# A hybrid mixer trunk on one core: the first norm's weights spread by TensorE, four weight tiles, convolutions that read a copy

## The chip, the core and the metric

The kernel runs on one core of a Trainium2 chip. Its engines each work through their own list of instructions in order: PE (TensorE: matmuls and transposes), DVE (VectorE), ACT (ScalarE), POOL (GpSimd), and SP (SyncE), which here only issues transfers (DMA). An instruction waits at the head of its engine's list until what it needs is there, and what stands behind it waits too. Matmuls write PSUM, which has eight banks of 128x512 f32; everything else lives in SBUF. The metric is the device time of one execution in microseconds (us), less is better.

## The reference

One layer on 512 tokens of width 1024, in f32:

```
u = rms_norm(x, mix_norm_g)
fa, fb, fc, fd, fg = split(u @ w_in)            # w_in: 1024 x 10528
rwkv7_mix(fa)   gla_mix(fb)   mlstm_mix(fc)     # fc: conv of 4 taps on q, k, then silu
ssd_mix(fd)                                     # z, xbc, dt; xbc: conv of 4 taps, then silu
merged = sum_i sigmoid(fg_i) * (branch_i @ branch_proj_i)
h = x + merged @ w_out
u = rms_norm(h, ffn_norm_g)
gate, val = split(conv3(u @ ffn_up))
out = rms_norm(h + (silu(gate) * val) @ ffn_down, final_norm_g)
```

`rms_norm(x, g)` is `x * rsqrt(mean(x*x) + eps) * g` over the 1024 columns; `g` is one row, the same for all tokens. A convolution of four taps is `y[t] = b + w3 x[t] + w2 x[t-1] + w1 x[t-2] + w0 x[t-3]` for each channel, and silu of it follows.

## The kernel before, in words

Tokens stand in four blocks of 128. The head (lines 287 to 298) loads `x` by block (`xt`), the norm's weights spread over 128 partitions (`g1`, a transfer of 512 KB, line 292), and then, for each block, squares on ACT (line 262), the inverse root on DVE and POOL (lines 247, 248), the product `un` on DVE (line 265), eight transposes on PE (line 269) and the split of the result in two parts, `uh` (a cast on ACT, line 251) and `ul` (the rest, a subtraction on DVE, line 252).

Each dense product with weights is a **split product**: a part of the weights, 128x512, arrives as `raw` (line 222, three buffers, issued by SP), ACT casts it to `hi` (line 225), DVE, or POOL for some, subtracts to `lo` (line 226), and PE does three matmuls for each chunk of 128 rows: lines 235 to 237 (128x512) for outputs that have channels on the partitions, lines 330 to 332 (128x256) for outputs that have tokens there. `hi` and `lo` have three buffers each (line 218). A part lives until its last matmul; then its pair is free for the part three later. Sums of dense products stand in the pool `psd` of three PSUM banks; `psr` (three) and `psm` (two) serve the rest, and `pm()` hands out `psm` or, in some stretches, by a running count, `psr`.

The stages, in the order of the profile: head; first half of rwkv, whose triangular solve is a chain of 62 DVE rows (lines 600, 602) that ends in a transfer to DRAM and back (`mnd`, `MN`) before PE's line 629; gla; the eight convolutions of ssd (`ssd_x`, which calls `conv4`, lines 902 to 912), two or three of them inside the first solve; ssd with its branch and the projection `z` (lines 1084, 1085, which read `psd` and so free its banks); the second half of rwkv with the second solve and the four convolutions of mlstm; mlstm; the output product; the FFN.

`conv4` reads the product's bank: ACT makes the fourth tap with the bias (line 904), three DVE instructions add the other taps (line 907), each with the bank as one input, ACT takes tanh (line 909), DVE finishes silu (line 910). In ssd, for each of four blocks `b`, a transfer spreads a row of cumulated decays over 128 partitions (`sab`, line 1019, 512 KB, two buffers), lines 1022 to 1043 make the decay factors on DVE, ACT and POOL, line 1052 multiplies by the scores, and PE multiplies by the inputs (line 1056).

The order of every engine's list is made by a scheduler that simulates the kernel with its own costs and takes, of the instructions that are ready, the one of highest priority; priorities stand in the table `Q` (lines `P_*`, and `split=800` for the casts and subtractions of weights). So a buffer more, or an instruction more, moves rows far from the edit.

Of the kernel before, what the change touches and what calls it, by code (L numbers as in the profile page):

```python
# [9 lines left out]
F32 = mybir.dt.float32  # L10
F32R = mybir.dt.float32r
AF = mybir.ActivationFunctionType
ALU = mybir.AluOpType
# [3 lines left out]
P = 128  # L17
T = 512
D = 1024
# [141 lines left out]
def kernel(ctx: ExitStack, tc: tile.TileContext, A, out):  # L161
    nc = tc.nc
    V, S, G, PE = nc.vector, nc.scalar, nc.gpsimd, nc.tensor
# [23 lines left out]
    wp = ctx.enter_context(tc.tile_pool(name="wp", bufs=1))  # L187
# [26 lines left out]
    def col(name, i=0, lo=0, hi=P):  # L214
        return pf[lo:hi, PF_AT[name] + i:PF_AT[name] + i + 1]

    def w_tiles():
        return (wp.tile([P, 512], F32R, tag="hi", name="hi", bufs=3), wp.tile([P, 512], F32R, tag="lo", name="lo", bufs=3))

    def split_h(src, h, tiles=None, eng=V):  # L220
        raw = wp.tile([P, 512], F32, tag="raw", name="raw", bufs=NRAW)
# [66 lines left out]
    xt = np_.tile([P, NB, D], F32, name="xt")  # L288
    g1 = np_.tile([P, D], F32, name="g1")
    nc.sync.dma_start(xt[:, 0], x_v[:, 0])  # L290
    nc.sync.dma_start(ident, A["cst"][:, 0:P])
    nc.sync.dma_start(g1, A["gvec"][0:D].partition_broadcast(P))
    for b in range(1, NB):
        nc.sync.dma_start(xt[:, b], x_v[:, b])
    for b in range(NB):
# [42 lines left out]
    def t2(pool=None):  # L338
        pl, n = pool or wpool
        return pl.tile([P, T], F32, tag="w", name="w", bufs=n)  # L340
# [559 lines left out]
        return res  # L900

    def conv4(ps, w, b, n, i, pool=None):
        y = t2(pool)
        S.activation(y, ps, AF.Identity, scale=col(w, 3 * n + i), bias=col(b, i))
        for k in range(3):
            d = 3 - k
            V.scalar_tensor_tensor(y[:, d:T], ps[:, 0:T - d], col(w, k * n + i), y[:, d:T], op0=ALU.mult, op1=ALU.add)  # L907
        th = t2(pool)
        S.activation(th, y, AF.Tanh, scale=0.5)
        V.scalar_tensor_tensor(y, th, 1.0, y, op0=ALU.add, op1=ALU.mult)  # L910
        return y
# [297 lines left out]
    nc.sync.dma_start(gb2, A["gvec"][D:2 * D].partition_broadcast(P))  # L1209
    gb3 = hp.tile([P, D], F32, name="gb3")  # L1210
    nc.sync.dma_start(gb3, A["gvec"][2 * D:3 * D].partition_broadcast(P))
    hw_ctx = ExitStack()
    hw = hw_ctx.enter_context(tc.tile_pool(name="hw", bufs=1, side="right", reuse_waits="tile"))
    wx = [hw.tile([P, 512], F32R, name=n) for n in ("wxh", "wxl")]
    hx = ExitStack()
    np_ = hx.enter_context(tc.tile_pool(name="nq", bufs=1, side="right", reuse_waits="tile"))

# [5 lines left out]
    for b in range(NB):  # L1223
# [3 lines left out]
        for n in range(2):  # L1227
            ps = pd()
            for k in range(KD):
                w = n * 8 + k  # L1230
# [5 lines left out]
        norm_T(h2[:, b], gb2, b, np_, uh, ul, 1, [pr_, pm])  # L1236
    tap("h2", h2)
    hx.close()
    first = fm_halves([(A["up"][0], (None, None)), (A["up"][1], (None, (wx[0], wx[1])))])
    hw_ctx.close()  # L1240
    wo_ctx.close()
    mo_ctx.close()
    ps_ctx.close()
# [91 lines left out]
```

## Time and profile before

| | |
|---|---|
| median of 3 runs | 1195.45 us (1193.54 to 1199.78) |
| profiled execution | 1195.54 us, its span 1193.7 us |
| busy, share of the span | PE 96%, DVE 55%, ACT 37%, POOL 28% |
| mean granted clock of PE | 0.984 of full |
| chain that ended last | PE 74%, DVE 11%, DMA 7%, issue 4%, ACT 2% |
| costliest rows | DVE line 226, 229.0 us; ACT line 225, 199.6 us; PE lines 235 to 237, 1073.7 us |

The profiled execution is 1.8 us longer than its span (start and end around it). A busy PE counts from a matmul's start to its modelled end, and neighbours overlap, so what PE loses is read from the bracket at the end of a row of the timeline: the idle time before that instruction, and what ended it. The clock column gives the share of full clock that was granted in a stretch.

### The profile page before, as it was taken

Reading aid. Unit: us, or ns where it says so; the run is one execution under the profiler, and the core shown is the slowest. Engines: PE = TensorE matmul, PEld = TensorE weight load, DVE = VectorE, ACT = ScalarE, POOL = GpSimd, SP = SyncE. Lnnn points to the kernel's source line nnn. Section 1 sums busy time; section 2 is a strip of 40 time slices with the busy share of each in tenths; the row PEclk is TensorE's granted clock in tenths of the full one; section 3 lists DMA queues with packets and bytes.
Section 4 is the critical chain, followed back from the end, with each engine's and each line's share of the span. In section 5 each row is a group of like instructions: output and inputs, shape, how many; then the busy total and the mean of one; then the engine's idle time right before and its main releaser. Section 6 shows DMA issues by size and latency. Waiting matters only on the chain.

```text
span 1193.7 us, 17895 instructions
## 1 busy us (share of the span) xinstructions
PE 1143.7 (96%) x6881; PEld 928.9 (78%) x6881; DVE 651.6 (55%) x1090; ACT 444.4 (37%) x820; POOL 331.4 (28%) x287
## 2 busy tenths in 40 slices
PE   5999989999999999989999999999999999999997
PEld 4887868777788767778777777778788888888886
DVE  5258796453576365793235653554665666652323
ACT  4355234332333432232124343432444444442323
POOL 3104012230285543331114543620212222220100
PEclk9999989999998999999999999999999999999999
DMA  5222322322341322332224523561232223222322
GB/s 198 65 98 64 88 61 70 103 78 79 105 98 53 98 80 67 93 83 91 68 84 150 160 88 115 184 201 38 89 101 96 96 96 99 97 97 97 97 97 107
DMA packets 79886, 117.30 MB, mean 98 GB/s; under 512 B 22660, under 2 KB 27172, under 8 KB 79800
## 3 DMA queue, kind: packets, MB, share of 16 engines
q1 hardware_dynamic: 79224, 115.11, 30.6%
q8 instruction: 54, 0.88, 0.3%
q10 hardware_dynamic: 576, 1.05, 0.2%
q14 instruction: 32, 0.26, 0.1%
HBM read 107.93 MB, written 8.19 MB: 97 GB/s over the span
## 4 chain that ended last, share of the span: by engine, by line
PE 74%; DVE 11%; DMA 7%; issue 4%; ACT 2%; POOL 1%; SPq 1%; POOLq 0%; DVEq 0%; ACTq 0%
PE psd L235 17%; PE psd L236 16%; PE psd L237 16%; PE psd L1282 3%; PE psd L1283 3%; PE psd L1284 3%; DVE Mi L602 2%; DVE Mt L600 2%; DMA sab<-ad 2%; DVE lo L226 1%; PE psr L676 1%; PE psd L331 1%; PE psd L330 1%; DMA raw<-in_wo_dram 1%; PE psd L332 1%
## 5 line engine op out<-in xcount | busy, mean ns | idle before, releaser
L226 DVE TENSOR_TENSOR lo<-raw,hi 128x512 fp32r<-128x512 f32 x280 | 229.0, 819 | 312.0 <-ACT hi L225 300.6
L225 ACT CAST hi<-raw 128x512 fp32r<-128x512 f32 x322 | 199.6, 620 | 485.7 <-PE psd L236 300.9
L235 PE MATMUL psd<-uh,hi 128*128 128x512 f32 (+1 forms) x912 | 359.9, 395 | 11.5 <-DVE w L907 4.8
L237 PE MATMUL psd<-uh,lo 128*128 128x512 f32 (+1 forms) x912 | 357.6, 393 | 4.5 <-DVE lo L226 4.1
L236 PE MATMUL psd<-ul,hi 128*128 128x512 f32 (+1 forms) x912 | 356.2, 391 | 0.2 <-DVE ul L252 0.2
L235 PEld LDWEIGHTS psd<-uh,hi 128*128 128x128 f32 x912 | 172.2, 189 | 53.0 <-ACT hi L225 6.2
L237 PEld LDWEIGHTS psd<-uh,lo 128*128 128x128 f32 x912 | 172.2, 189 | 44.8 <-DVE lo L226 5.6
L236 PEld LDWEIGHTS psd<-ul,hi 128*128 128x128 f32 x912 | 172.3, 189 | 36.8 <-issue 2.6
L226 POOL TENSOR_TENSOR lo<-raw,hi 128x512 fp32r<-128x512 f32 x42 | 56.9, 1356 | 194.2 <-ACT hi L225 157.5
L1271 POOL TENSOR_TENSOR y<-y 128x512 f32<-128x512 f32 x22 | 28.3, 1288 | 174.0 <-DVE y L1265 160.1
L1265 DVE SCALAR_TENSOR_TENSOR y<-psd,pf,y 128x510 f32<-128x510 f32 x88 | 65.9, 750 | 2.7
L1284 PE MATMUL psd<-hi,al 128*128 128x512 f32 x164 | 63.8, 389 | 0.0
L1283 PE MATMUL psd<-lo,ah 128*128 128x512 f32 x164 | 63.8, 389 | 0.0
L331 PE MATMUL psd<-lo,uh 128*128 128x256 f32 x192 | 57.1, 298 | 1.0 <-DVE lo L226 1.0
L1282 PE MATMUL psd<-hi,ah 128*128 128x512 f32 x164 | 57.3, 389 | 0.0
L332 PE MATMUL psd<-hi,ul 128*128 128x256 f32 x192 | 56.3, 294 | 0.0
L330 PE MATMUL psd<-hi,uh 128*128 128x256 f32 x192 | 55.8, 292 | 0.0
L331 PEld LDWEIGHTS psd<-lo,uh 128*128 128x128 f32 x192 | 37.8, 197 | 5.2 <-issue 3.3
L332 PEld LDWEIGHTS psd<-hi,ul 128*128 128x128 f32 x192 | 37.9, 197 | 1.3 <-issue 1.0
L330 PEld LDWEIGHTS psd<-hi,uh 128*128 128x128 f32 x192 | 37.7, 197 | 1.6 <-issue 1.2
L1284 PEld LDWEIGHTS psd<-hi,al 128*128 128x128 f32 x164 | 30.8, 188 | 6.5
L1282 PEld LDWEIGHTS psd<-hi,ah 128*128 128x128 f32 x164 | 30.8, 188 | 6.4
(418 smaller groups left out, 1696.5 us busy)
## 6 DMA issues: line engine op xcount, KB each, us to landing
raw<-in_wfm_dram SPq DMA_DIRECT2D x140, 256.0 KB, 2.6
raw<-in_up_dram SPq DMA_DIRECT2D x88, 256.0 KB, 2.5
raw<-in_dn_dram SPq DMA_DIRECT2D x44, 256.0 KB, 2.5
raw<-in_bp_dram SPq DMA_DIRECT2D x32, 256.0 KB, 2.7
raw<-in_wtm_dram SPq DMA_DIRECT2D x24, 256.0 KB, 2.6
raw<-in_wo_dram SPq DMA_DIRECT2D x16, 256.0 KB, 3.0
gd<-th SPq DMA_DIRECT2D x15, 256.0 KB, 2.1
th<-gd SPq DMA_DIRECT2D x15, 256.0 KB, 2.9
```

What stands on the lines that cost most here:

```text
L225: S.copy(hi, raw)
L226: eng.tensor_tensor(lo, raw, hi.bitcast(F32), op=ALU.subtract)
L235: PE.matmul(ps, lh, rh, start=first, stop=False)
L236: PE.matmul(ps, lh, rl, start=False, stop=False)
L237: PE.matmul(ps, ll, rh, start=False, stop=last)
L330: PE.matmul(o, uh[:, k, bs], hi[:, cs], start=first, stop=False)
L331: PE.matmul(o, uh[:, k, bs], lo[:, cs], start=False, stop=False)
L332: PE.matmul(o, ul[:, k, bs], hi[:, cs], start=False, stop=last)
L1265: V.scalar_tensor_tensor(y[:, d:T], ps[:, 0:T - d], col("fcw", k * 44 + n), y[:, d:T], op0=ALU.mult, op1=ALU.add)
L1282: PE.matmul(ps, ah[:, k, bs], hi, start=(k == 0), stop=False)
L1283: PE.matmul(ps, ah[:, k, bs], lo, start=False, stop=False)
L1284: PE.matmul(ps, al[:, k, bs], hi, start=False, stop=(k == NF - 1))
```

## The change

Three edits.

1. The row of the norm's weights comes as one row (`grow`, 4 KB) in place of the spread copy of 512 KB. A row of ones times it, two f32 products on PE, spreads it in two PSUM banks (one of `psd`, one of `psm`), and DVE copies both into `g1`.
2. `hi` and `lo` have four buffers each. The extra pair `wx` that held one part of the FFN's first product is gone; that part takes its tiles from the four.
3. `conv4` copies the bank to SBUF on ACT first (into `th`, the tile that takes the tanh later), and the four taps read the copy. ACT has one more instruction of 128x512 for each of the twelve convolutions; the bank is free after that copy.

```diff
--- before.py
+++ after.py
@@ -215,7 +215,7 @@
         return pf[lo:hi, PF_AT[name] + i:PF_AT[name] + i + 1]
 
     def w_tiles():
-        return (wp.tile([P, 512], F32R, tag="hi", name="hi", bufs=3), wp.tile([P, 512], F32R, tag="lo", name="lo", bufs=3))
+        return (wp.tile([P, 512], F32R, tag="hi", name="hi", bufs=4), wp.tile([P, 512], F32R, tag="lo", name="lo", bufs=4))
 
     def split_h(src, h, tiles=None, eng=V):
         raw = wp.tile([P, 512], F32, tag="raw", name="raw", bufs=NRAW)
@@ -288,8 +288,15 @@
     xt = np_.tile([P, NB, D], F32, name="xt")
     g1 = np_.tile([P, D], F32, name="g1")
     nc.sync.dma_start(xt[:, 0], x_v[:, 0])
+    grow = np_.tile([1, D], F32, name="grow")
+    nc.sync.dma_start(grow, A["gvec"][0:D].partition_broadcast(1))
     nc.sync.dma_start(ident, A["cst"][:, 0:P])
-    nc.sync.dma_start(g1, A["gvec"][0:D].partition_broadcast(P))
+    ones = np_.tile([1, P], F32, name="ones")
+    V.memset(ones, 1.0)
+    for n, bank in enumerate((pd, pm)):
+        ps = bank()
+        PE.matmul(ps, ones, grow[:, n * 512:(n + 1) * 512], start=True, stop=True)
+        V.tensor_copy(g1[:, n * 512:(n + 1) * 512], ps)
     for b in range(1, NB):
         nc.sync.dma_start(xt[:, b], x_v[:, b])
     for b in range(NB):
@@ -900,12 +907,12 @@
         return res
 
     def conv4(ps, w, b, n, i, pool=None):
-        y = t2(pool)
-        S.activation(y, ps, AF.Identity, scale=col(w, 3 * n + i), bias=col(b, i))
+        y, th = t2(pool), t2(pool)
+        S.copy(th, ps)
+        S.activation(y, th, AF.Identity, scale=col(w, 3 * n + i), bias=col(b, i))
         for k in range(3):
             d = 3 - k
-            V.scalar_tensor_tensor(y[:, d:T], ps[:, 0:T - d], col(w, k * n + i), y[:, d:T], op0=ALU.mult, op1=ALU.add)
-        th = t2(pool)
+            V.scalar_tensor_tensor(y[:, d:T], th[:, 0:T - d], col(w, k * n + i), y[:, d:T], op0=ALU.mult, op1=ALU.add)
         S.activation(th, y, AF.Tanh, scale=0.5)
         V.scalar_tensor_tensor(y, th, 1.0, y, op0=ALU.add, op1=ALU.mult)
         return y
@@ -1209,9 +1216,6 @@
     nc.sync.dma_start(gb2, A["gvec"][D:2 * D].partition_broadcast(P))
     gb3 = hp.tile([P, D], F32, name="gb3")
     nc.sync.dma_start(gb3, A["gvec"][2 * D:3 * D].partition_broadcast(P))
-    hw_ctx = ExitStack()
-    hw = hw_ctx.enter_context(tc.tile_pool(name="hw", bufs=1, side="right", reuse_waits="tile"))
-    wx = [hw.tile([P, 512], F32R, name=n) for n in ("wxh", "wxl")]
     hx = ExitStack()
     np_ = hx.enter_context(tc.tile_pool(name="nq", bufs=1, side="right", reuse_waits="tile"))
 
@@ -1236,8 +1240,7 @@
         norm_T(h2[:, b], gb2, b, np_, uh, ul, 1, [pr_, pm])
     tap("h2", h2)
     hx.close()
-    first = fm_halves([(A["up"][0], (None, None)), (A["up"][1], (None, (wx[0], wx[1])))])
-    hw_ctx.close()
+    first = fm_halves([(A["up"][0], (None, None)), (A["up"][1], (None, None))])
     wo_ctx.close()
     mo_ctx.close()
     ps_ctx.close()
```

Below, rows of the engines' lists. Line numbers of after are 7 higher from the head's loop on, names carry other numbers.

The head on DVE (`un` is the normed block, `ul` its low part; `omu` to `dskip` are small constants for later, made from the transfers `pf` and `dskip`). Before:

```order
L265 SCALAR_TENSOR_TENSOR un_144<-xt_89,ss_140,g1_90 128x1024
L265 SCALAR_TENSOR_TENSOR un_165<-xt_89,ss_161,g1_90 128x1024
L252 TENSOR_TENSOR ul_85<-psr_125,uh_84 128x4x128
L354 TENSOR_SCALAR omu_313<-pf_77 128x14
L356 TENSOR_SCALAR hwa_315<-pf_77 128x8
L358 TENSOR_SCALAR oka_317<-pf_77 128x4
L360 TENSOR_SCALAR hng_319<-pf_77 128x1
L361 TENSOR_SCALAR hng_319<-pf_77 128x4
L438 COPY rkb_336<-pf_77 128x256
L351 TENSOR_SCALAR dskip_310<-dskip_310 128x8
```

After:

```order
L265 SCALAR_TENSOR_TENSOR un_111<-xt_89,ss_107,g1_90 128x1024
L265 SCALAR_TENSOR_TENSOR un_132<-xt_89,ss_128,g1_90 128x1024
L247 TENSOR_SCALAR ss_149<-ss_149 128x1
L361 TENSOR_SCALAR omu_322<-pf_77 128x14
L363 TENSOR_SCALAR hwa_324<-pf_77 128x8
L365 TENSOR_SCALAR oka_326<-pf_77 128x4
L367 TENSOR_SCALAR hng_328<-pf_77 128x1
L368 TENSOR_SCALAR hng_328<-pf_77 128x4
L445 COPY rkb_345<-pf_77 128x256
L358 TENSOR_SCALAR dskip_319<-dskip_319 128x8
L265 SCALAR_TENSOR_TENSOR un_153<-xt_89,ss_149,g1_90 128x1024
```

The two copies into `g1` stand ahead of these rows, and the seven rows from `omu` to `dskip`, which stood behind the fourth `un`, now stand ahead of the third.

The middle of ssd on SP (`ad` is the row of decays in DRAM, `sab` its spread copy, the four in order of the blocks; `in_wtm` are the weights of `z`, `in_wfm` those of the next stage). Before:

```order
L1019 DMA sab_2738<-ad_2725 128x8x128
L1019 DMA sab_2795<-ad_2725 128x8x128
L222 DMA raw_3464<-in_wtm_dram 128x512
L222 DMA raw_3470<-in_wtm_dram 128x512
L222 DMA raw_3524<-in_wtm_dram 128x512
L222 DMA raw_3530<-in_wtm_dram 128x512
L222 DMA raw_3594<-in_wtm_dram 128x512
L1019 DMA sab_2858<-ad_2725 128x8x128
L222 DMA raw_3600<-in_wtm_dram 128x512
L222 DMA raw_3654<-in_wtm_dram 128x512
L222 DMA raw_3660<-in_wtm_dram 128x512
L1019 DMA sab_2921<-ad_2725 128x8x128
```

After:

```order
L222 DMA raw_3677<-in_wtm_dram 128x512
L1013 DMA ad_2742<-w_2738 8x512
L1026 DMA sab_2755<-ad_2742 128x8x128
L1026 DMA sab_2812<-ad_2742 128x8x128
L222 DMA raw_3793<-in_wfm_dram 128x512
L222 DMA raw_3799<-in_wfm_dram 128x512
L222 DMA raw_3833<-in_wfm_dram 128x512
L1026 DMA sab_2875<-ad_2742 128x8x128
L1026 DMA sab_2938<-ad_2742 128x8x128
```

The weights of `z` used to be issued between the four `sab`; now all of them stand ahead of `ad`, and the third and fourth `sab` are neighbours.

The same place on DVE (`sf_2923` before and `sf_2940` after are the factors of the fourth block; lines 1085 and 1092 read a bank of `psd` for `z`). Before:

```order
L1050 COPY sbt_2891<-psm_2890 128x256
L1052 SCALAR_TENSOR_TENSOR sab_2858<-psr_2889,sab_2858 128x512 x2
L226 TENSOR_TENSOR lo_3603<-raw_3600,hi_3602 128x512
L1063 TENSOR_TENSOR w_2875<-psr_2910,sf_2860 128x512
L1074 TENSOR_TENSOR w_2918<-w_2918,psr_2915 128x512
L1033 COPY w_2936<-psr_2931 128x512
L1058 TENSOR_TENSOR w_2873<-w_2873,psm_2899 128x512
L1038 TENSOR_TENSOR w_2938<-w_2936,sf_2923 128x512
L1085 SCALAR_TENSOR_TENSOR w_3458<-w_3458,psd_3462 128x256
```

After:

```order
L1031 TENSOR_SCALAR sf_2940<-sf_2940 128x8
L1032 TENSOR_TENSOR sf_2940<-sab_2938,stk_2753 128x8
L1040 COPY w_2953<-psm_2948 128x512
L1048 TENSOR_SCALAR sab_2938<-sab_2938,stk_2753 128x128
L1045 TENSOR_TENSOR w_2955<-w_2953,sf_2940 128x512
L1034 SCALAR_TENSOR_TENSOR sf_2940<-sf_2940,stk_2753 128x8
L1048 TENSOR_SCALAR sab_2938<-sab_2938,stk_2753 128x128 x3
L1092 SCALAR_TENSOR_TENSOR w_3475<-w_3475,psd_3479 128x256
L1092 SCALAR_TENSOR_TENSOR w_3475<-w_3475,psd_3609 128x256
L1102 TENSOR_TENSOR w_2770<-w_2770,w_3475 128x512
L1092 SCALAR_TENSOR_TENSOR w_3476<-w_3476,psd_3479 128x256
L1092 SCALAR_TENSOR_TENSOR w_3477<-w_3477,psd_3480 128x256
```

The first reader of a `z` bank stood behind the third block's line 1052; now it stands right behind the fourth block's factors, and the third block's line 1059 (1052 before) comes behind all of them.

The same place on PE, behind the second block's products with `sab` (line 1056 before, 1063 after). Before:

```order
L1031 MATMUL psr_2868<-cst_76,w_2301 128x128
L1048 MATMUL psr_2889<-w_2436,w_2346 128x128
L1048 MATMUL psr_2889<-w_2481,w_2391 128x128
L331 MATMUL psd_3462<-lo_3527,uh_84 128x256
L332 MATMUL psd_3462<-hi_3526,ul_85 128x256
L330 MATMUL psd_3462<-hi_3526,uh_84 128x256
L331 MATMUL psd_3462<-lo_3527,uh_84 128x256
L332 MATMUL psd_3462<-hi_3526,ul_85 128x256
L330 MATMUL psd_3462<-hi_3526,uh_84 128x256
L331 MATMUL psd_3462<-lo_3527,uh_84 128x256
```

After:

```order
L1063 MATMUL psm_2853<-w_2829,sab_2812 128x64 x4
L1056 MATMUL psm_2907<-cst_76,w_2359 128x128
L1056 MATMUL psm_2907<-cst_76,w_2405 128x128
L1038 MATMUL psm_2948<-cst_76,w_2175 128x128
L1038 MATMUL psm_2948<-cst_76,w_2221 128x128
L1038 MATMUL psm_2948<-cst_76,w_2267 128x128
L1038 MATMUL psm_2948<-cst_76,w_2313 128x128
L1055 MATMUL psm_2969<-w_2451,w_2359 128x128
L1055 MATMUL psm_2969<-w_2497,w_2405 128x128
L337 MATMUL psd_3610<-hi_3613,uh_84 128x256
```

Before, split products of `z` (`psd_3462`) fill the place between the blocks; now only small products do, and the next split product opens a bank of its own, `psd_3610`, after `psd_3479`, `psd_3480` and `psd_3609`, so it needs one of these three freed.

## Rows read from the trace of the kernel before

**Rows 1.** The page, part 2: PE and its clock in 40 slices.

```profile
PE   5999989999999999989999999999999999999997
...
PEclk9999989999998999999999999999999999999999
```

**Rows 2.** Busy time by stretch; columns in the first line.

```profile
core 0: us, PE busy (x) PEld busy (x) DVE busy (x) ACT busy (x) POOL busy (x), PEclk, DMA share, GB/s
...
150.00:165.00 15.00, 10.16 (x128) 7.76 (x127) 14.76 (x30) 5.07 (x9) 3.87 (x3) 0.77 0.15 54
...
300.00:330.00 30.00, 28.67 (x148) 22.12 (x147) 18.03 (x37) 10.34 (x23) 10.28 (x9) 1.00 0.31 98
...
330.00:375.00 45.00, 41.76 (x281) 38.95 (x279) 31.48 (x59) 12.15 (x24) 35.06 (x29) 0.92 0.30 76
...
510.00:525.00 15.00, 12.54 (x48) 9.91 (x47) 14.35 (x27) 3.66 (x6) 6.41 (x5) 0.89 0.25 88
```

**Rows 3.** Waits: who waited for whom, us in total, times, longest.

```profile
ACT hi L225 <- PE psd L236: 300.9, 174, 6.2
```

**Rows 4.** Head, 0 to 25 us: start, duration, instruction, idle before it.

```profile
1.64 0.42 SPq L292 DMA_DIRECT2D g<-in_gvec_dram  x1
...
8.89 1.29 DVE L265 SCALAR_TENSOR_TENSOR un<-xt,ss,g 128x1024 f32<-128x1024 f32 x1 [3.27 <-DMA g<-in_gvec_dram]
...
19.41 0.64 DVE L354 TENSOR_SCALAR omu<-pf 128x14 f32<-128x14 f32 x1
...
23.47 0.15 DVE L351 TENSOR_SCALAR dskip<-dskip 128x8 f32<-128x8 f32 x1
...
10.18 1.06 ACT L262 ACTIVATE sq<-xt 128x1024 f32<-128x1024 f32 x1 [4.76 <-DMA xt<-in_x_dram]
...
24.27 0.39 PE L236 MATMUL psd<-ul,wh 128*128 128x256 f32 x1 [1.29 <-DVE ul L252]
```

**Rows 5.** Line 460: a 128x512 f32 product, as two records; ns min, median, max.

```profile
L460 PE MATMUL psm<-w,cst x8: 592/592/593, 45.7 to 402.9; 128*4 128x512 f32 x8
```

**Rows 6.** PE, matmuls that came late behind a wait for hi or lo.

```profile
94.03 0.39 PE L331 MATMUL psd<-lo,uh 128*128 128x256 f32 x1 [1.02 <-DVE lo L226]
...
328.64 0.50 PE L235 MATMUL psd<-uh,hi 128*128 128x512 f32 x1 [0.76 <-ACT hi L225]
...
441.21 0.54 PE L235 MATMUL psd<-uh,hi 128*128 128x512 f32 x1 [1.77 <-ACT hi L225]
...
502.38 0.50 PE L237 MATMUL psd<-uh,lo 128*128 128x512 f32 x1 [0.88 <-DVE lo L226]
...
516.03 0.50 PE L237 MATMUL psd<-uh,lo 128*128 128x512 f32 x1 [2.46 <-DVE lo L226]
```

**Rows 7.** PE behind the first convolution, and behind the second solve.

```profile
158.72 0.80 PE L235 MATMUL psd<-uh,hi 128*128 128x512 f32 x1 [4.78 <-DVE w L907]
...
533.95 0.22 PE L629 MATMUL psr<-MN,zm 32*32 32x32 f32 x2 [0.62 <-DMA MN<-mnd]
```

**Rows 8.** Lines 907 and 910: duration ns min, median, max, forms.

```profile
L907 DVE SCALAR_TENSOR_TENSOR w<-psd,pf,w x36: 728/748/751, 155.8 to 544.4; 128x509 f32<-128x509 f32 x12, 128x510 f32<-128x510 f32 x12, 128x511 f32<-128x511 f32 x12
...
L910 DVE SCALAR_TENSOR_TENSOR w<-w x12: 657/693/1727, 161.4 to 545.9; 128x512 f32<-128x512 f32 x12
```

**Rows 9.** The solve on DVE, and POOL beside it.

```profile
505.13 0.42 DVE L602 TENSOR_TENSOR Mi<-Mi,Mt 64x256 f32<-64x256 f32 x1
...
507.95 1.40 DVE L600 TENSOR_TENSOR Mt<-Ls,Mi 64x252 f32<-64x252 f32 x1
...
507.60 1.48 POOL L226 TENSOR_TENSOR lo<-raw,hi 128x512 fp32r<-128x512 f32 x1
```

**Rows 10.** SSD: the fourth broadcast of sab, DVE's wait, PE's wait.

```profile
351.45 0.39 SPq L1019 DMA_DIRECT2D sab<-ad  x1
...
357.01 0.99 DVE L1025 TENSOR_TENSOR sf<-sab,stk 128x8 f32<-128x8 f32 x1 [3.34 <-DMA sab<-ad]
...
360.66 1.76 PE L1056 MATMUL psm<-w,sab 128*128 128x64 f32 x7 [3.24 <-DVE sab L1052]
```

## The prediction, made before the run

> **What bounds the kernel now.** I read the page's slices first. PE is at nine tenths nearly everywhere and its clock is full but for single slices [rows 1], so time can be won only where PE idles, in the head, and where a stall is followed by the lower clock level. The stretches come next [rows 2]: from 150 to 165 us PE is busy 10.16 of 15 us at a mean clock of 0.77, from 330 to 375 us 41.76 of 45 at 0.92, from 510 to 525 us 12.54 of 15 at 0.89. The timelines of PE then give the single stalls with what ended them [rows 6, 7, 10]. The waits say what the weights' casts wait for: 300.9 us of ACT's waiting is for a matmul that still reads the pair of three parts before [rows 3]; it is slack of ACT, and costs only where PE then waits for hi or lo. In the last 12 slices PE is at nine tenths or more but for the end [rows 1], with no stall that the change touches, so I give the FFN nothing; that one part takes its tiles from the ring costs nothing either, as the ring is one pair longer.
>
> My sum is made against the profiled execution, 1195.5 us (span 1193.7 and 1.8 around it), which is the median of the runs.
>
> **Edit 1, the head.** It removes a transfer of 512 KB, issued at 1.64 us, whose landing releases the first un at 8.89 us after 3.27 us of waiting by DVE; the second block of x lands at 10.18 us, behind it [rows 4]. It adds a 4 KB transfer, two f32 products (each as two records of 0.59 us, so at most 1.2 us a product [rows 5]) and two copies. A copy of 128x512 from PSUM I take at 0.74 us, from the taps that read PSUM [rows 8]. If the row lands as late as the first un's other input allows (8.89 − 3.27 = 5.6 us is when DVE was idle before), products and copies end at some 7.5 us, and the first un starts 1.4 us earlier; at best the whole 3.27 us is won, and as much again if the blocks of x, which shared the transfer engines with the 512 KB, land earlier too: −4.5. Against it stands the new order on DVE: seven rows from omu to dskip now run ahead of the third un. They took from 19.41 to 23.6 us [rows 4], 4.2 us, and wait for transfers of their own, so the third un loses part of what the first gained. The head's last wait, 1.29 us before 24.27 us, after which PE streams, is for ul, behind the same DVE rows. I take −1.5, with −4.5 and +2 as ends.
>
> **Edit 2, a fourth pair.** Five stalls wait for hi or lo: 1.02 + 0.76 + 1.77 + 0.88 + 2.46 = 6.9 us [rows 6]. A part of weights feeds 12 matmuls, whose records are about 0.5 us long [rows 6] and overlap by some half, so a part lasts about 3 us (an estimate), and the fourth pair lets a cast start that much earlier. Each of the five is shorter than that, so I take all: −7. Where a stall goes, the lower clock behind it may go too: from 510 to 525 us a clock of 0.89 means 15 × 0.11 = 1.7 us of work lost, which makes −8.5 the low end. The other end is 0: two of the five lie inside the second solve, where lo stands in DVE's list among the solve's rows (14.35 of 15 us busy [rows 2]), and a free buffer does not make DVE free.
>
> **Edit 3, the convolutions.** PE waits 4.78 us before 158.72 us because the three taps of the first convolution, behind rows of the solve, still read the bank that the next product needs [rows 7]. ACT's 1.06 us for 128x1024 [rows 4] make some 0.6 us for a copy of half that; with it on ACT, busy 5.07 of 15 us there [rows 2], the bank is free after 0.6 us: 4.8 us gone, and with it the lower clock (15 × 0.23 = 3.45 us of work): −8.2 at most. But PE next needs the solve's result. Before, it waits only 0.62 us for it at 533.95 us [rows 7], so PE and the solve arrive nearly together, and a faster PE waits longer there. By the order DVE runs 104 rows from the solve's first to its last, before 99: three more taps, at 0.75 us each, one more silu row and one more lo, some 3 us more. PE has about 5 us more of dense products ahead of line 629 in the new order, which fills most of that. So of 8.2 us I count −2.5, with −8.2 and +3 as ends. The twelve copies on ACT (7 us in all, ACT 37% busy) are hidden beside PE's products of the next parts; the four of mlstm would cost 4 × 0.6 = 2.4 us where that cover is gone, as PE's line for the scores waits for them.
>
> The taps themselves change one input from PSUM to SBUF. Before, they took 728 to 751 ns, in all 36 cases, while line 910, with two inputs in SBUF, took 657 to 1727 ns [rows 8], and a row of the solve with two SBUF inputs went from 0.42 to 1.40 us while POOL ran beside it [rows 9]. So a tap costs 0.66 us without POOL and up to 1.73 us beside it; POOL is busy 3.87 of 15 us in the first convolutions' stretch [rows 2], so on average it is near 0.9. I keep 0.75 in the sum and give the worse case to a rival. The Trainium skill, SBUF — State Buffer, section "Who interferes with whom", says that a VectorE instruction with two SBUF inputs contends with a GpSimd instruction that reads SBUF, and one with at most one SBUF input doesn't; this trace agrees, by the three rows just named, and by that rule the edit puts 36 instructions under contention that were free of it. Its page VectorE: DVE Perf Modes, section "Rules for kernel authors", says the opposite for a case like this: copy PSUM to SBUF first if many operations follow. No row here has that gain beyond 0.09 us a tap, 3 us of DVE in all.
>
> **What moves: ssd.** This is the largest term, and none of the edits is made there. Before, PE has work of z between the blocks: from 300 to 375 us it idles 1.3 + 3.2 us [rows 2], nearly all of it 3.24 us before 360.66 us, where the third block waits for line 1052, which stands behind a factor of the fourth block, which waits for the fourth sab (issued 351.45, landed 357.01, 5.6 us) [rows 10]. In the new order the weights of z are loaded ahead of the decays, their products are mostly done when the second block's products with sab run, and behind these PE has eight small products and then needs a bank that holds z. Its readers on DVE and ACT stand behind the fourth block's factors, so behind the fourth sab, which can be issued only when the second block's buffer is free. That is a chain: issue and landing 5.6 to 6 us, the factor 0.2 to 1.0 us, the decays and the other rows ahead of the first reader 2 to 3 us, readers of the bank 1 to 2 us: about 10 us in which PE has about 1 us of work. I take 10 us of idle here and 3.5 us before the first block (less of z is left to cover its chain too), 13.5, less the 4.5 of before: +9. The lower clock behind it stands in before as well (45 × 0.08 = 3.6 us of work). Ends: 0 if the order's small products come late enough to be cover themselves, +15 if the first blocks' chains are uncovered too.
>
> **Sum.** −1.5 − 7 − 2.5 + 9 = −2; 1195.5 − 2 = 1193.5 us.
>
> **Rivals.**
> - *The gain stays.* PE reaches ssd later relative to the transfers than I think, and idles there little more than before (+2 in place of +9): −1.5 − 7 − 2.5 + 2 = −9, 1186.5 us. For it: sab's chain begins at the rwkv and gla stage, not at PE, and transfers land in 5.6 us. Against: the z products stand ahead of the blocks by the order, whatever the time.
> - *ssd idles long (the other side).* The fourth sab's wait holds z's banks, and the first blocks' chains are open as well: +15 there, and the weights' stalls inside the second solve stay (−3.5 in place of −7), the convolutions give 0: −1.5 − 3.5 + 15 = +10, 1205.5 us. It decides from some 13 us of added idle between 300 and 375 us. For it: three neighbours on SP and two stages of DVE behind one transfer. Against: before, PE needed only 3.24 us more of that transfer.
> - *Taps beside POOL.* Six taps in the first solve at 1.7 us in place of 0.75 make it 6 us longer, and PE waits for it at line 629: 1193.5 + 6 = 1199.5 us. POOL's share there, a quarter, speaks against all six.
> - *Nothing comes of it*: late weights are DVE's own lateness, the bank's wait turns into the wait for the solve, z finds cover: 1195.5 us.
>
> **How the numbers follow.** Chances: forecast 0.42 (its own range 1187 to 1199), gain stays 0.26 (1179 to 1189), ssd idles long 0.18 (1202 to 1211), taps beside POOL 0.08 (1196 to 1203), nothing 0.06. No measurement of this kernel tells less than 0.5%, 6 us, from no change: faster is below 1189.5, slower above 1201.4. Faster: 0.26 and a fifth of the forecast, 0.35. Slower: 0.18 and a third of the taps, 0.21. The range 1181 to 1206 leaves out the outer third of the second case and of the third.
>
> **What would show it.** Right: first un below 8 us; no wait for hi or lo above 0.5 us before 840 us; no wait of PE for a tap; line 629's first row behind a wait of 2 to 5 us for MN; between 300 and 375 us (about the same work) one idle of PE of 7 to 12 us, ended by a reader of a z bank. Wrong: if that idle is under 4 us the time is below 1189; if it is above 14 us, or the taps' mean is above 1.2 us, it is above 1200.

## The result, and the profile after

The changed kernel takes 1226.86 us (median of 4 runs, 1226.35 to 1229.36) against 1194.49 us before (1192.93 to 1199.78, 4 runs): 2.7% slower, ratio 1.0267 with the 95% interval [1.0232, 1.0303]. The forecast was 1193.5 us in a range of 1181 to 1206, so it was wrong by 33 us; the rival that went the right way, at 1205.5, was 21 us short.

The slices of PE and its clock in the page of after; the twelfth to fifteenth slices (338 to 460 us) stand at 8, 5, 8 and 7, and the clock at 8, 7, 9 and 8. In [rows 1] PE stands at 9 in all four, and the clock too but for an 8 in the thirteenth:

```profile
PE   6998989999985879998999999999999999999997
...
PEclk9998989999987989998999999999999999999999
```

Two groups of dense matmuls (busy, mean ns of one, idle before them and what ended most of it), line 237 before, then lines 235 and 237 from part 5 of the page of after:

```profile
L237 PE MATMUL psd<-uh,lo 128*128 128x512 f32 (+1 forms) x912 | 357.6, 393 | 4.5 <-DVE lo L226 4.1
```

```profile
L235 PE MATMUL psd<-uh,hi 128*128 128x512 f32 (+1 forms) x920 | 362.4, 396 | 15.0 <-DVE w L431 5.8
L237 PE MATMUL psd<-uh,lo 128*128 128x512 f32 (+1 forms) x920 | 359.4, 392 | 1.3 <-DVE lo L226 1.3
```

PE's waits for lo of DVE before line 237 fell to 1.3 us in all (4.1 before), so the fourth pair did what it was to do there. The idle before line 235 has another cause now, line 431, the token shift of rwkv's second half, which reads a bank of dense products.

To see where the time went I took two landmarks that both kernels have: the first half's last chunk of rwkv (line 681 before, 688 after) and the first row of the second half's preparation (line 509, 516). PE's timeline, before and then after:

```profile
302.80 0.40 PE L681 MATMUL psr<-st,kr 64*64 64x64 f32 x8
431.43 1.09 PE L509 MATMUL psr<-wa,wau 64*64 64x512 f32 x8
```

```profile
324.83 0.40 PE L688 MATMUL psr<-st,kr 64*64 64x64 f32 x8
467.39 1.09 PE L516 MATMUL psr<-wa,wau 64*64 64x512 f32 x8
```

The last chunk comes 22.0 us late and the second half 36.0 us late, more than the whole loss; from there on PE wins 2 us back. The split products that PE ran ahead of the second landmark are the same in both (291.9 and 292.1 us of them, by the records of the traces), so these 36 us are lost time and not moved work. The stretch between the landmarks, busy time by engine (columns as in [rows 2]), before and after:

```profile
303.00:431.00 128.00, 123.28 (x685) 104.28 (x680) 73.81 (x134) 47.39 (x98) 69.22 (x56) 0.97 0.31 91
```

```profile
325.00:467.00 142.00, 112.87 (x604) 95.58 (x601) 68.71 (x126) 43.85 (x91) 66.70 (x56) 0.87 0.22 70
```

I price such a stretch as PE's idle time plus its length times what is missing of the clock. Before: 128 − 123.28 = 4.7 and 128 × 0.03 = 3.8, together 8.6 us. After: 142 − 112.87 = 29.1 and 142 × 0.13 = 18.5, together 47.6 us. That is an upper price, as idle time at the lower clock counts in both, but the stretch with these 39 us between them is where the result was made. The single stalls, in PE's timeline of after:

```profile
356.26 0.58 PE L337 MATMUL psd<-hi,uh 128*128 128x256 f32 x1 [5.91 <-DVE mg L418]
...
377.75 0.47 PE L1056 MATMUL psm<-cst,w 128*128 128x128 f32 x1 [3.82 <-DVE w L1065]
...
382.72 0.58 PE L1055 MATMUL psm<-w 128*128 128x128 f32 x1 [2.65 <-DVE w L1040]
...
388.51 0.58 PE L337 MATMUL psd<-hi,uh 128*128 128x256 f32 x1 [4.56 <-DVE w L1092]
...
427.61 0.79 PE L235 MATMUL psd<-uh,hi 128*128 128x512 f32 x1 [3.18 <-DVE w L1092]
...
445.29 0.80 PE L235 MATMUL psd<-uh,hi 128*128 128x512 f32 x1 [5.78 <-DVE w L431]
```

The first four lie ahead of ssd's first block and between its blocks, where before had one stall of 3.24 us [rows 10]. The first, 5.91 us, waits for line 418, which stands in DVE's list behind a wait of 5.01 us for the first `sab`; the fourth is the reader of a `z` bank that the prediction named. The last two lie behind ssd, where the prediction saw nothing. DVE's timeline shows what stood ahead of line 431:

```profile
444.41 0.17 DVE L473 TENSOR_SCALAR nn<-nn 128x16 f32<-128x16 f32 x1 [10.31 <-DMA nn<-nq]
444.49 0.74 DVE L431 SCALAR_TENSOR_TENSOR w<-psd,pf,w 128x511 f32<-128x511 f32 x1
```

Line 431, which frees a bank for the next product, stands in DVE's list behind a row that waits 10.31 us for a transfer to DRAM and back (`nn<-nq`). Before, DVE waited 0.33 us for the same transfer (line 466, at 407.13 us), and PE had no wait above 0.8 us from 361 to 441 us.

The head, on DVE, in order of time, to be set beside [rows 4]:

```profile
6.73 0.69 DVE L299 COPY g<-psd 128x512 f32<-128x512 f32 x1 [1.06 <-PE psd L298]
...
8.39 0.15 DVE L247 TENSOR_SCALAR ss<-ss 128x1 f32<-128x1 f32 x1 [0.96 <-ACT sq L262]
8.46 0.68 DVE L299 COPY g<-psm 128x512 f32<-128x512 f32 x1
9.24 2.48 DVE L265 SCALAR_TENSOR_TENSOR un<-xt,ss,g 128x1024 f32<-128x1024 f32 x2
...
13.43 2.26 DVE L265 SCALAR_TENSOR_TENSOR un<-xt,ss,g 128x1024 f32<-128x1024 f32 x1
```

The first product `un` comes at 9.24 us, not below 8 (8.89 before): the second copy into `g1` stands behind row 247 of the second block, which waits for ACT until 8.39 us. PE was ahead all the same at 40 us: it had done 18.2 us of split products, 16.9 before. Then a new wait of 1.56 us before 59.31 us, for `sg` (line 454), took this back, and by 80 us the head has gained nothing.

### The profile page after: what moved, and what is told of

It reads as the page before. It is cut to its first block, busy times and chain, and to the rows that moved or that the text cites. A ratio compares the mean times of both kernels' runs of the same rounds, so it can differ in the third digit from the quotient of the medians.

```text
span 1227.6 us, 17906 instructions
## 1 busy us (share of the span) xinstructions
PE 1152.6 (94%) x6885; PEld 938.5 (76%) x6885; DVE 658.9 (54%) x1093; ACT 452.4 (37%) x832; POOL 333.5 (27%) x287
## 5 line engine op out<-in xcount | busy, mean ns | idle before, releaser
L235 PEld LDWEIGHTS psd<-uh,hi 128*128 128x128 f32 x920 | 175.2, 191 | 55.5 <-DVE w L431 6.7
L237 PEld LDWEIGHTS psd<-uh,lo 128*128 128x128 f32 x920 | 174.9, 190 | 38.6 <-DVE lo L226 2.2
L236 PEld LDWEIGHTS psd<-ul,hi 128*128 128x128 f32 x920 | 175.3, 190 | 36.7 <-issue 2.1
L337 PE MATMUL psd<-hi,uh 128*128 128x256 f32 x192 | 59.2, 308 | 10.5 <-DVE mg L418 5.9
L1285 PE MATMUL psd<-hi,ah 128*128 128x512 f32 x164 | 63.8, 389 | 0.0
L339 PE MATMUL psd<-hi,ul 128*128 128x256 f32 x192 | 59.4, 310 | 0.0
L337 PEld LDWEIGHTS psd<-hi,uh 128*128 128x128 f32 x192 | 40.3, 210 | 14.3 <-DVE mg L418 6.3
L1286 PEld LDWEIGHTS psd<-lo,ah 128*128 128x128 f32 x164 | 30.8, 188 | 6.4
```

The lines of the kernel that those rows point to most:

```text
L235: PE.matmul(ps, lh, rh, start=first, stop=False)
L236: PE.matmul(ps, lh, rl, start=False, stop=False)
L237: PE.matmul(ps, ll, rh, start=False, stop=last)
L337: PE.matmul(o, uh[:, k, bs], hi[:, cs], start=first, stop=False)
L339: PE.matmul(o, ul[:, k, bs], hi[:, cs], start=False, stop=last)
L1285: PE.matmul(ps, ah[:, k, bs], hi, start=(k == 0), stop=False)
```

## The experiments

Two kinds of numbers recur. The time and its ratio to the kernel before on the same chip (medians of 1195.1 to 1195.9 us there), with the 95% interval in brackets. And the **dense work ahead of the chain**: split products that stand in PE's list ahead of rwkv's last chunk of the first half, counted and priced at the spacing that PE keeps (0.227 us for 128x512, 0.12 us for 128x256). It is 198.9 us before and 217.5 us after; the records of the traces, a few of which are missing, give 198.0 and 216.4.

**Each part alone.** In one line each, from the diff of the change: the head's hunk; the pairs with `wx` gone; `conv4`; the first and the third together.

```diff
+    nc.sync.dma_start(grow, A["gvec"][0:D].partition_broadcast(1))        # head
+        return (wp.tile([P, 512], F32R, tag="hi", name="hi", bufs=4), ...)  # pairs
+        S.copy(th, ps)                                                       # convolutions
```

> Only the head's edit (one row of weights, two products, two copies). Theory A (the fourth pair of weight tiles alone moves the dense products ahead and costs the 32 us): near before, 1190 to 1197 us, and PE starts ssd's last products with sab near 375 us as before. Theory B (the head's additional bank shifts the running count of pm() and so the banks of ssd, which makes the loss): above 1210 us, with the loss between 330 and 450 us.

> Only the four pairs of hi and lo (and no wx). Theory A: the whole loss, 1222 to 1232 us, with some 217 us of dense work in PE's list ahead of the first half of rwkv's last chunk in place of 199, and 20 us or more lost from 330 to 460 us. Theory B (head's banks) or theory C (the convolutions' copy): below 1205 us.

> Only the convolutions' copy. Theory A: near before or a little faster, 1188 to 1197 us: the stall of 4.8 us at the first convolution is gone and the lower clock behind it, part of it comes back at line 629. Theory C (the longer solve and taps beside POOL make the loss): above 1205 us, taps' mean above 1.0 us.

> Head and convolutions, three pairs as before. Theory A: the sum of both alone, 1186 to 1196 us, at least 28 us under the changed kernel. Theories B, C, or that the three edits only lose together: above 1205 us.

Measured: head 1207.82 us (1.0098 [1.0077, 1.0119]), pairs 1229.43 (1.0278 [1.0257, 1.0300]), convolutions 1197.78 (1.0019 [1.0004, 1.0033]), head and convolutions 1202.75 (1.0064 [1.0030, 1.0097]; its runs lie from 1197.06 to 1209.96). The pairs alone make the whole loss. No part wins anything, and they do not add up: +12.5, +34 and +2.5 alone, +32 together. Theory A, that the pairs make the loss, gave the right time for the pairs; its times for the head (to 1197) and for head and convolutions (to 1196) were missed by 11 and 7 us, that for the convolutions by 1. That the head alone costs 12 us is near what B said, and was followed up below.

**What of the pairs costs.** Four pairs, but each part's pair is fixed: every fourth part takes the fourth pair by name (the count starts anew at each stage), where a ring of four gives whichever is free. With head and convolutions, and without:

```diff
+        wn[0] += 1
+        if four[0] and wn[0] % 4 == 0:
+            return (wp.tile([P, 512], F32R, tag="hx", name="hi", bufs=1), ...)
-        return (wp.tile([P, 512], F32R, tag="hi", name="hi", bufs=4), ...)
+        return (wp.tile([P, 512], F32R, tag="hi", name="hi", bufs=3), ...)
```

> All three edits with four pairs, but every fourth part of the weights is given the fourth pair by name, in place of one ring that takes whichever is free. By the order, 201.9 us of dense work then stand ahead of the first half's last chunk of rwkv (198.9 before, 217.5 in the changed kernel). Theory A (the ring of four lets dense products overtake the rwkv chain, and the work is missing later as cover in ssd and behind it): 1198 to 1210 us. Theory D (four pairs cost by themselves, whatever the order: casts and subtractions ahead of the chain on ACT and DVE): 1220 to 1232 us.

> The kernel before with four pairs alone, every fourth part given the fourth pair by name (the head and the convolutions as before). By the order, 201.0 us of dense work stand ahead of the first half's last chunk of rwkv (217.3 with the ring of four, 198.9 before). Theory A (place of the rwkv chain in the dense work): 1194 to 1206 us, at least 23 us under four pairs in one ring (1229.43). Theory D (four pairs cost by themselves): 1220 us or more.

Measured: 1210.15 us (1.0128 [1.0113, 1.0144]) and 1205.15 us (1.0095 [1.0065, 1.0125]): the same number of pairs, 17 and 24 us less than with the ring. Theory D falls for most of the loss, but 10 us stay with the fixed pairs. In the second kernel they are lost by the end of the first solve, not in ssd:

```profile
100.00:120.00 20.00, 17.99 (x83) 12.09 (x84) 10.48 (x18) 7.53 (x12) 3.78 (x5) 0.57 0.10 23
```

The clock is 0.57 there (0.91 before, in the same 20 us). It fell behind a wait of 2.01 us before 102.01 us, and then PE, busy again, ran rwkv's preparation in small products with few dense ones between. This part goes with the fourth pair itself: waits of 1.68 and 2.0 us at 95 to 104 us stand in every kernel whose fourth pair is in use by then, ring or not, and in none with three pairs. Priced as above, from 80 to 130 us these kernels lose 8.0 to 12.9 us, the kernel before 3.5.

Then two kernels that keep the changed kernel's ring of four and all three edits, and change only when some loads of weights may start. In the first the loads of `z` wait for ssd's decays; in the second those of the branch's outputs 4 to 7 and of `z` wait for the rwkv state behind the seventh of eight chunks. Both by a copy of one element into the raw tile ahead of its load:

```diff
         raw = wp.tile([P, 512], F32, tag="raw", name="raw", bufs=NRAW)
+        if gate_:
+            V.tensor_copy(raw[0:1, 0:1], gate_[0])
         nc.sync.dma_start(raw, src[:, 512 * h:512 * h + 512])
```

> The changed kernel, but each load of z's weights waits for the transposed decays of ssd (a copy of one element into the raw tile, from these decays, ahead of each load), so that z's products stand between the blocks of ssd; the rwkv chain's place stays (217.5 us of dense work ahead of it). Theory A: ssd gets cover back and the stalls of 13 us between 366 and 389 us shrink, the wait between the rwkv chain's end and ssd's first block grows: 1212 to 1222 us, 5 to 15 us under the changed kernel. Theory D: no change, 1223 to 1230 us.

> The changed kernel with its ring of four; the loads of weights for the branch's outputs 4 to 7 and for z wait for the rwkv state behind the first half's seventh chunk (a copy of one element of it into the raw tile ahead of each load). By the order 193.7 us of dense work stand ahead of the last chunk, in place of 217.5, and split products of z stand between the blocks of ssd as before. Theory A (the dense work that overtakes the chain is missing as cover in ssd and behind it): 1197 to 1209 us, and from the chain's end to the second half's preparation some 16 to 22 us are lost by PE in place of 47. Theory D (something else that four pairs or the edits bring): 1220 us or more.

Measured: 1225.3 us (1.0265 [1.0226, 1.0304]), no better; and 1208.18 us (1.0119 [1.0085, 1.0153]), 19 us better, in theory A's range. Holding `z` alone leaves the chain where it was in the dense work (217.5 us), and mostly moves the loss: priced as above, 8.7 us more from 330 to 360 us and 11.8 us less from 360 to 390 us. That was a miss of my expectation, and it taught what counts: not which product is kept for ssd, but how much. Holding the branch too brings the chain to 193.7 us of dense work, and it ends at the time of the kernel before (line 691 is 681 there):

```profile
303.57 0.40 PE L691 MATMUL psr<-st,kr 64*64 64x64 f32 x8
```

The same stretch, from the chain's end to the second half's preparation, in this kernel, in the pairs alone, in the fixed pairs alone, and with `z` held:

```profile
304.00:446.00 142.00, 130.81 (x702) 110.73 (x703) 80.30 (x156) 51.19 (x104) 69.86 (x56) 0.95 0.31 94
```

```profile
329.00:469.00 140.00, 114.65 (x616) 97.16 (x614) 66.46 (x126) 44.62 (x91) 68.01 (x56) 0.89 0.25 73
```

```profile
319.00:447.00 128.00, 122.87 (x676) 104.21 (x671) 72.19 (x132) 47.85 (x98) 69.47 (x57) 0.96 0.30 89
```

```profile
325.00:464.00 139.00, 111.08 (x613) 93.50 (x613) 70.68 (x134) 44.40 (x91) 66.88 (x56) 0.90 0.25 76
```

Priced as above: 11.2 + 7.1 = 18.3 us, 25.4 + 15.4 = 40.8, 5.1 + 5.1 = 10.2, 27.9 + 13.9 = 41.8. Set beside the dense work ahead of the chain:

| kernel | dense work ahead | chain ends at | second half at | lost between | time |
|---|---|---|---|---|---|
| before | 198.9 | 303 | 431 | 8.6 | 1195 |
| fixed pairs alone | 201.0 | 319 | 447 | 10.2 | 1205.2 |
| convolutions alone | 198.7 | 312 | 441 | 9.7 | 1197.8 |
| head alone | 198.9 | 309 | 442 | 13.9 | 1207.8 |
| changed, fixed pairs | 201.9 | 313 | 446 | 16.1 | 1210.2 |
| changed, branch and z held | 193.7 | 304 | 446 | 18.3 | 1208.2 |
| pairs in a ring alone | 217.3 | 329 | 469 | 40.8 | 1229.4 |
| changed, z held | 217.5 | 325 | 464 | 41.8 | 1225.3 |
| changed | 217.5 | 325 | 467 | 47.6 | 1226.9 |

The stretches are of one execution, the times are medians; the execution of the changed kernel was its slowest (1229.36), that of `z` held its fastest (1223.3). The three kernels with 217 us lose 41 to 48 us there, all others at most 18. All have run 292 us of dense work by the start of the second half, so what they are late there is lost: 36 us in the changed kernel, 33 and 38 in the other two with 217 us, 10 to 16 in the rest. Behind it some win a part back: from there to the end the table's kernels take 756 to 765 us, the kernel before 762. The kernel with branch and `z` held keeps 12 us of loss although its chain has the least work ahead. They lie in this very stretch: its chain ends 1 us late and its second half starts 15 us late, with 5.2 us of dense work moved into the stretch (198.9 − 193.7) and 9.7 us more lost there (18.3 − 8.6), with waits of 2.65 us for a cast of weights and of 3.59 and 2.84 us in ssd. So the work ahead of the chain separates the two groups and does not order the kernels inside one.

How I read it: a pair that is free lets the scheduler put dense products ahead of chain steps that it takes for not ready. On the chip PE worked through the chain's stretch without idle either way (busy 39.90 of 40 us from 220 to 260 us before, 40.00 after), so the 18.6 us spent there bought nothing, and they are missing where PE waits for transfers: in ssd and behind it.

**The count of banks.** The head draws one more bank from `pm()`, whose running count decides which banks ssd uses. The count alone, in the kernel before; then, with -1 in place of 1, the head without the shift, and head and convolutions without it:

```diff
-    wide, turn = [False], [0]
+    wide, turn = [False], [1]
```

> The kernel before with nothing but the running count of pm() started one higher, as the head's additional bank does; the rest of the work is the same. Theory B in its small form (the count moves the banks of ssd, and this is most of the 12 us that the head's edit alone costs): 1200 to 1207 us, with new stalls between 355 and 370 us. Theory E (the 12 us come from the place of line 629, 116.0 us of dense work ahead of it in place of 111.7): 1193 to 1198 us.

> The head's edit alone with the count of pm() started one lower, so that ssd's banks are handed out as before. Theory E (the head's 12 us come from the place of line 629 and the order behind it, not from banks): 1203 to 1209 us. Theory B: 1194 to 1199 us.

> Head and convolutions, three pairs, and the count of pm() started one lower, so that banks are handed out as before. Dense work ahead of the first half's last chunk is 193.7 us, the least of all orders so far. Theory A: the rwkv chain ends earlier and more cover is left for ssd: 1188 to 1197 us, under head and convolutions with the shifted count (1202.75). Theory E: no better than that, 1199 to 1206 us, as line 629 stands behind 117.6 us of dense work in both.

Measured: 1196.5 us (1.0011 [0.9997, 1.0026]), 1200.18 us (1.0046 [1.0027, 1.0065]) and 1204.68 us (1.0077 [1.0060, 1.0093]). The count costs nothing by itself and some 7 us beside the head, and its undoing does not help head and convolutions. The first and the third time are those of theory E, the second fits neither theory.

The traces say where the head's 12 us lie. Its chain ends 6 us late, with as much dense work ahead as before, and 5.5 of these are a lower clock with no idle of PE:

```profile
180.00:230.00 50.00, 50.00 (x533) 41.45 (x532) 24.40 (x47) 18.25 (x33) 8.08 (x5) 0.86 0.28 72
```

Before, the same 50 us are as busy at 0.97. In the head's kernel line 636 (629 before) stands behind 116.0 us of dense work (111.7 before), and from 183.08 to 188.48 us PE runs small products alone:

```profile
183.08 1.09 PE L833 MATMUL psm<-w 32*64 32x128 f32 x16
184.10 0.37 PE L636 MATMUL psr<-MN,zm 32*32 32x32 f32 x10
...
187.55 0.65 PE L848 MATMUL psm<-w 64*32 64x32 f32 x32
...
188.48 0.80 PE L235 MATMUL psd<-uh,hi 128*128 128x512 f32 x1
189.07 0.63 PE L236 MATMUL psd<-ul,hi 128*128 128x512 f32 x1
```

The clock averages 0.73 from 185 to 190 us and 0.58 from 190 to 195, and a dense product behind them takes 0.63 us in place of 0.39. Before, dense products from 180.98 to 185.5 us stand between these small ones, and the clock is 1.00. A second 5 us are lost from the chain's end to the second half, in waits of 1.53 and 4.23 us in ssd and 1.87 us behind it. The count alone has the same waits (1.43, 4.23 and 1.87 us) and a second half that starts 5.3 us late, but it is back at the time of before by the end of the execution; the rows here do not say by what.

The same clock tells why head and convolutions without the shift missed its time. By the order its chain has the least dense work ahead (193.7 us); on the chip the chain ends at 314 us, as it does with the shift, and the clock from 180 to 230 us is 0.69 there and 0.83 with the shift. So the dense work ahead of the chain does not rank orders that lie close together. Whether dense products between the small ones would win this back was not tried.

**The convolutions' wait.** In the convolutions' kernel PE no longer waits for the bank; it waits for a row of gla that stands in DVE's list behind rows of the solve. I gave POOL more of DVE's work there:

```diff
-    ... L_x=1 ...
+    ... L_x=3 ...
```

> The convolutions' copy alone, and both subtractions of each convolution's weights on POOL in place of one, so that DVE has eight fewer rows of 128x512 in the stretch of the first solve. If PE's wait there is DVE's list (the bank's wait turned into a wait for gla's row behind the solve, 4.99 us before 165.65 us), that wait shrinks by 2 us or more and line 629 comes earlier than 189 us: 1190 to 1196 us. If POOL's extra work slows the solve's rows (0.4 to 1.4 us): 1198 to 1204 us.

Measured: 1198.73 us (1.0033 [1.0015, 1.0051]), no better than the 1197.78 without it: the second case of the expectation. PE's stall in the first solve, first in the convolutions' kernel and then with POOL's help:

```profile
165.65 3.79 PE L854 MATMUL psm<-w 128*128 128x128 f32 x16 [4.82 <-DVE w L845]
```

```profile
168.46 1.86 PE L854 MATMUL psm<-w 128*128 128x128 f32 x7 [7.57 <-DVE w L845]
```

It grew from 4.82 to 7.57 us: POOL was busy 12.31 in place of 9.90 us from 125 to 175 us, and the solve's rows of lines 600 and 602 in that window took 26.1 us for 58 rows in place of 22.3 for 56.

**A version that beats both.** The fixed fourth pair only from the second half's projections on, on the kernel before without the other edits (`wx` is gone here too), so that everything ahead keeps its order; and the same with the third branch's subtractions all on POOL:

```diff
+    four[0], wn[0] = True, 0      # ahead of the second half's projections, of the third branch, of mlstm, of the output, of the FFN
+        if four[0] and wn[0] % 4 == 0:      # the fourth pair, as above
-    ... L_br3=2 ...      # the second kernel only
+    ... L_br3=3 ...
```

> The kernel before with the fourth pair by name from the second half of rwkv's projections on; everything ahead of that is the order of before, row for row. If the late parts behind hi and lo are worth their stalls (1.8, 0.9 and 2.5 us and a lower clock level behind two of them) and nothing is moved into a worse place: 1188 to 1193 us. If the second solve and what follows gives it back: 1194 to 1198 us.

> The version with the fourth pair by name from the second half of rwkv's projections on (1189.67 us), and both subtractions of each part of the third branch's weights on POOL in place of one. If the stall of 4.2 us in the second solve is lo behind the solve's rows on DVE: 1184 to 1188 us. If POOL, slower and in the way of DVE's rows with two inputs in SBUF, gives it back: 1189 to 1195 us.

Measured: 1189.67 us (0.9966 [0.9949, 0.9982]) and 1194.1 us (0.9995 [0.9977, 1.0012]). The first is 5 us faster than the kernel before and 37 us faster than the changed one: a fourth pair pays where the order around it holds. Its dearest stall from the second half on is in the second solve:

```profile
517.84 0.80 PE L242 MATMUL psd<-uh,lo 128*128 128x512 f32 x1 [4.00 <-DVE lo L231]
```

In the second kernel this wait is still for a lo of DVE, 4.31 us before 522.16 us: the subtraction that PE waits for is not one of those given to POOL, and the gain is gone.

## Why the prediction was wrong

**The step that failed** is "What moves: ssd ... +9", with ends 0 and +15. The chain of waits that it names is in the trace: z's weights ahead of the decays, a reader of z's bank behind the fourth sab, PE without a product. Its size was wrong in three ways. From 330 to 390 us PE idles 18.3 us (busy 41.70 of 60), where I had 13.5: 5.91 before the first block for my 3.5, and 3.82 + 2.65 + 4.56 = 11.0 between the blocks for my 10. The rows on DVE ahead of the first reader took 7.7 us (378.82 to 386.51), not 2 to 3, with one of line 1045 at 2.84 us while POOL ran (0.68 to 1.08 in the other blocks). The stretch behind ssd, to 467 us, I left out, and it has stalls of 3.18 and 5.78 us and the lower clock. And "the lower clock behind it stands in before as well" was false: 18.5 us of work lost to it, against 3.8 before. By the upper price above the stretch cost 39 us more, and I had 9. The sign that I gave for being wrong, an idle above 14 us there and a time above 1200, is what came.

The cause was also not the place of z. With z held back until ssd the stretch still lost 41.8 us. What was missing was 18.6 us of dense work that had gone ahead of the rwkv chain, and the prediction does not count it. I read the order at the place where it looked worst and priced that; the question was what the whole stretch to the next full supply of dense work would run on.

**The cause was put at the wrong edit's door, or at none.** I gave the fourth pair −7 for five late parts, and the moved order no owner. The pairs alone cost 34 us. The five stalls for lo and hi did go: none of 0.8 us or more is left in the changed kernel (line 237's fell from 4.1 to 1.3 us in all), so the term's mechanism was right. No run shows that it is worth 7 us. The late fixed pair, 5 us in all, lost the wait of 1.77 us and the lower clock behind it, but its wait of 2.46 us grew to 4.00; some 3 us more came from 534 to 551 us, where no wait for lo or hi stood and the clock rose from 0.93 to 1.00. The price of the pair stood elsewhere in the list.

**The convolutions, −2.5.** The bank's stall of 4.78 us went, and another of the same length took its place 7 to 10 us later: 4.45 us before 169.03 us, behind gla's row on DVE. I had followed PE to line 629 and passed over a reader in between. Alone the edit is +0.2%. The wait that I named at line 629 (636 after) came in the second half only:

```profile
571.70 0.28 PE L636 MATMUL psr<-MN,zm 32*32 32x32 f32 x2 [5.36 <-DMA MN<-mnd]
```

It was 0.62 us before [rows 7]. But the convolutions do not make it: alone they have no wait of 0.8 us or more there, and the pairs alone have one of 4.49 us.

**The taps beside POOL**, a rival at 0.08, were real but small:

```profile
L915 DVE SCALAR_TENSOR_TENSOR w<-w,pf 128x509 f32<-128x509 f32 (+2 forms) x36 | 30.5, 848 | 3.1 <-ACT w L912 2.6
```

The mean rose from 744 ns (728 to 751, [rows 8]) to 848: 36 × 0.104 = 3.7 us of DVE. Four taps took 1631 to 1770 ns, each while POOL ran; the other 32 took 733 to 753, so the copy itself gained nothing, and the 0.66 that I took from line 910 does not hold for a tap. This agrees with the Trainium skill, SBUF — State Buffer, section "Who interferes with whom": an instruction with two SBUF inputs can be held up by GpSimd, one with a PSUM input was not. The estimate "near 0.9" for the mean was right.

**The head, −1.5**, was near the truth up to 40 us, where PE was 1.3 us ahead, and no further: line 516 comes at 79.93 us, and before, as line 509, at 79.59. That was luck, as the way there was not the one I gave: the second copy waits behind a row for the second block, the seven small rows are cheap (1.0 us, not 4.2), and the third `un` takes 2.26 us beside POOL (1.28 before). That the order behind it moves, and costs 12 us alone, is not in the prediction; why the scheduler moved it stays open.

**The chances.** I gave slower 0.21 and the range ended at +10 us. A change that moves hundreds of rows of a list deserved a far wider upper end than a sum over ten named stalls gives; the two edits that looked local were not.

## What to carry to other kernels

When a list is made by a scheduler, one more buffer is not a local edit: count, at a few landmarks of the longest chain, how much independent work stands ahead of each, before and after. Independent work that moves ahead of a chain which did not wait is lost as cover for the next place that does. Where a buffer is wanted for one stretch, give it to that stretch by name and keep the order elsewhere.

## What the runs showed of the hardware

The granted clock fell to its lower level (1.2 of 2.4 GHz) not only behind waits. In the head's kernel PE was busy 50.00 of 50 us from 180 to 230 us, and the clock averaged 0.86: it fell while PE ran products of 32x128, 32x32 and 64x32 alone from 183.08 us on, and was back at 1.00 from 195 to 210 us, behind dense products. In the fixed pairs' kernel it fell behind a wait of 2.01 us and averaged 0.57 from 100 to 120 us with PE busy 17.99 of 20. So a busy share of PE does not show that a stretch runs at full clock; the clock column has to be read beside it.
